# Stick-breaking attention: who carries the running product from one key chunk to the next

## The chip, the core and the metric

The kernel runs on one core of one Trainium2 chip. It is a single launch; the host only lays the arrays out. The metric is the device time of a run in microseconds (us). A profiled execution gives, beside its own time, the span from its first to its last instruction and a record of every instruction on the engines: TensorE (PE, with its weight loads PEld), VectorE (DVE), ScalarE (ACT), GpSimd (POOL) and the queue of SyncE (SP) that issues the DMAs.

## The reference, cut to what matters

One layer of a trunk: RMS norm with modulation, one wide input projection, a convolution branch, an attention branch, two gates, an output projection. Only the attention branch is touched. It is not a softmax: each query walks back over the earlier keys and leaves to each key a part of what is left.

```python
z = jnp.einsum("bqhd,bkhd->bhqk", qb, kb) * scale
mask = s_idx < t_idx
log_beta = jax.nn.log_sigmoid(z)
log_1m_beta = jnp.where(mask, log_beta - z, 0.0)
suffix = lax.cumsum(log_1m_beta, axis=3, reverse=True) - log_1m_beta
weights = jnp.where(mask, jnp.exp(log_beta + suffix), 0.0)
outs.append(jnp.einsum("bhqk,bkhd->bqhd", weights, vb))
```

Sequence 2048, 8 heads of 64, float32. The weight of a key is sigmoid(z) times the product of sigmoid(-z) over all keys between it and the query.

## The kernel before, in words

The sequence is laid out backwards, so that the product over the keys between becomes a running product from left to right. Heads are taken one after the other; in a head the queries come in 4 chunks `rc` of 512, and for each the key chunks `g` from `rc` to 3. So a head has ten **units** (rc, g): four on the diagonal (g = rc) and six off it, 80 in all. A unit has four query blocks `qb` of 128 rows.

`z_stage` (L783) does one query block of one unit: two matmuls give z in PSUM (L802, L803; the pool has two such buffers); ScalarE makes w = sigmoid(z) in SBUF (L805) and overwrites z by sigmoid(-z) in PSUM (L806); a scan on VectorE (L811, or L815 on the diagonal) writes the running product into columns 1 to 512 of `sc[qb]`, a tile of 513 columns of which there is one for each query block; GpSimd multiplies w by columns 0 to 511 of it (L818), and on the diagonal masks a 128x128 corner (L820). Column 0 holds what the chunk before has left. Off the diagonal a copy of one column on VectorE, L810, brings column 512 to column 0 before the scan. Its target is read by the product of the chunk before, so it cannot run until that product is done.

`av_stage` (L825) works on the unit before: TensorE transposes w into PSUM (L834, through the helper at L127), ScalarE casts it to `thi` (L842), VectorE makes the rest `tlo` (L843), and `av_mm` (L847) multiplies both by v and adds into `av`.

Between these stand filler matmuls: the dense projections of the merge gates, in steps of three matmuls (L763, tile `pd`), handed out over the quarters of the units by the list `due` (L949 to L954), which gives lighter units a little more. Of the fillers there are 416 steps, 402 of them inside the 302 quarters before `LAST`; in the last 18 quarters the first chunk of the next stage stands in their place.

The loop at L963 writes the order: Z(0), fillers, the held-back av_mm, fillers, Z(1), T(3), fillers, T(2), fillers, Z(2), fillers, AV(3), T(1), AV(2), T(0), Z(3), fillers, AV(1). With `pin[0]` set (L559) TensorE's matmuls keep this order (helpers `mm` and `tr`, L121 to L129). The queues of VectorE, ScalarE and GpSimd are ordered by the framework's planner, by what it takes to be ready and then by the place in the program; an instruction can stand in a queue well ahead of its place in the program. Each engine works its own queue off in order.

Of the kernel before, what the change touches and what calls it, by code (L numbers as in the profile page):

```python
# [22 lines left out]
CH = 512  # L23
NCH = SEQ // CH
# [21 lines left out]
def f(ap):  # L46
    return ap.bitcast(F32)
# [3 lines left out]
def trunk_kernel(  # L51
# [20 lines left out]
    nc = tc.nc  # L72
# [48 lines left out]
    def mm(*a, **k):  # L121
        i = nc.tensor.matmul(*a, **k)  # L122
        if pin[0]:
            tc.keep_in_program_order(i)
# [57 lines left out]
    with ExitStack() as s1:  # L182
# [193 lines left out]
        with tc.tile_pool(name="hx", reuse_waits="tile", bufs=1) as hx:  # L376
# [9 lines left out]
            for o in range(0, D, CH):  # L386
                s = slice(o, o + CH)
# [349 lines left out]
    with ExitStack() as s2:  # L737
# [37 lines left out]
        def load_q(h, rc):  # L775
            q1 = at.tile([P, CH], F32R, tag="q1", name="q1", bufs=2)
            q2 = at.tile([P, CH], F32R, tag="q2", name="q2", bufs=2)
            nc.sync.dma_start(f(q1), qst_d[h][rc])
            nc.sync.dma_start(f(q2[0:HD]), qst_d[h][rc][HD:P])
            nc.sync.dma_start(f(q2[HD:P]), qst_d[h][rc][0:HD])  # L780
            st[h, rc] = {"q": (q1, q2), "w": {}}

        def z_stage(h, rc, g, qb):  # L783
            diag = g == rc
            if qb == 0:
                if rc == 0:
                    kt[g] = at.tile([P, CH], F32R, tag=f"kt{g}", name=f"kt{g}")
                    nc.sync.dma_start(f(kt[g]), kst_d[h][g])
                    vt[g] = at.tile([P, 4, P], F32R, tag=f"vt{g}", name=f"vt{g}")
                    nc.sync.dma_start(f(vt[g]), vst_d[h][g])  # L790
                if diag:
                    nxt = (h, rc + 1) if rc + 1 < NCH else (h + 1, 0)
                    for hr in ((h, rc), nxt) if n_ == 0 else (nxt,):
                        if hr[0] < NH:
                            load_q(*hr)
            s_ = st[h, rc]
            q1, q2 = s_["q"]
            lo = qb * P if diag else 0
            zlo = min(lo, 256)
            qs = slice(qb * P, (qb + 1) * P)  # L800
            z = pz.tile([P, CH], F32, tag="z", name="z")
            mm(z[:, zlo:], q1[:, qs], kt[g][:, zlo:], start=True, stop=False)  # L802
            mm(z[:, zlo:], q2[:, qs], kt[g][:, zlo:], start=False, stop=True)  # L803
            w = at.tile([P, CH], F32, tag="w", name="w", bufs=7)
            nc.scalar.activation(out=w[:, lo:], in_=z[:, lo:], func=AF.Sigmoid, scale=HD ** -0.5)  # L805
            nc.scalar.activation(out=z[:, lo:], in_=z[:, lo:], func=AF.Sigmoid,  # L806
                                 scale=-HD ** -0.5)
            s = sc[qb]
            if not diag:
                nc.vector.tensor_copy(s[:, 0:1], s[:, CH:CH + 1])  # L810
                nc.vector.tensor_tensor_scan(  # L811
                    out=s[:, 1:], data0=z, data1=w, initial=s[:, 0:1],
                    op0=ALU.mult, op1=ALU.bypass)
            else:
                nc.vector.tensor_tensor_scan(  # L815
                    out=s[:, lo + 1:], data0=z[:, lo:], data1=tri[:, :CH - lo], initial=1.0,
                    op0=ALU.mult, op1=ALU.max)
            nc.gpsimd.tensor_tensor(out=w[:, lo:], in0=w[:, lo:], in1=s[:, lo:CH], op=ALU.mult)  # L818
            if diag:
                nc.gpsimd.affine_select(  # L820
                    out=w[:, lo:lo + P], in_=w[:, lo:lo + P], pattern=[[1, P]],
                    compare_op=ALU.is_gt, fill=0.0, base=0, channel_multiplier=-1)
            s_["w"][g, qb] = w

        def av_stage(h, rc, g, kb, v_):  # L825
# [137 lines left out]
        for n_, u in enumerate(units + [None]):  # L963
# [11 lines left out]
            def Z(qb):  # L975
                if u is not None:
                    z_stage(*u, qb)
# [118 lines left out]
```

## Time and profile before

| | us |
|---|---|
| median of three runs | 1952.85 |
| the three runs | 1952.85, 1944.73, 1953.7 |
| the profiled execution, its own time | 1947.37 |
| its span | 1945.6 |
| attention stage, about | 810 to 1602 of the span |

In the rows below, a group has its line, engine, operation, tiles (out<-in) and shape, then its count, its busy time, the mean of one in ns, and the idle time of its engine just before it with what ended that idle time. A row of the waits says who waited for whom, then us in total, how many times and the longest. A row of the chain gives start, duration and what; the chain is followed back from the last instruction to whatever released each one. A row of the windows gives a stretch, its length, and for each engine busy us and the count of instructions. A busy TensorE is not one at its peak, since its matmuls overlap and their ends are modelled.

### The profile page before, as it was taken

Reading aid. Unit: us, or ns where it says so; the run is one execution under the profiler, and the core shown is the slowest. Engines: PE = TensorE matmul, PEld = TensorE weight load, DVE = VectorE, ACT = ScalarE, POOL = GpSimd, SP = SyncE. Lnnn points to the kernel's source line nnn. Section 1 sums busy time; section 2 is a strip of 40 time slices with the busy share of each in tenths; the row PEclk is TensorE's granted clock in tenths of the full one; section 3 lists DMA queues with packets and bytes.
Section 4 is the critical chain, followed back from the end, with each engine's and each line's share of the span. In section 5 each row is a group of like instructions: output and inputs, shape, how many; then the busy total and the mean of one; then the engine's idle time right before and its main releaser. Section 6 shows DMA issues by size and latency. Waiting matters only on the chain.

```text
span 1945.6 us, 27211 instructions
## 1 busy us (share of the span) xinstructions
PE 1823.4 (94%) x9612; PEld 1517.2 (78%) x9612; DVE 1248.5 (64%) x1947; ACT 809.5 (42%) x1988; POOL 667.6 (34%) x739
## 2 busy tenths in 40 slices
PE   5889999999999989999998999999989889999999
PEld 4777898998988977777776777676767667888887
DVE  6864678787787445267776767676777797333341
ACT  3761122231221122266666666666667664010100
POOL 6441111011011144356465656455655551010100
PEclk9999999999999999999999999999999999999999
DMA  7335114052142444423232323131313246453532
GB/s 246 135 107 176 43 28 136 17 167 78 45 140 71 152 146 156 145 90 88 62 89 63 92 66 91 57 95 58 103 55 101 69 152 205 138 153 101 162 97 77
DMA packets 115290, 206.88 MB, mean 106 GB/s; under 512 B 15185, under 2 KB 27473, under 8 KB 115154
## 3 DMA queue, kind: packets, MB, share of 16 engines
q1 hardware_dynamic: 115154, 205.14, 33.8%
q8 instruction: 76, 1.25, 0.3%
q14 instruction: 60, 0.49, 0.1%
HBM read 133.78 MB, written 71.30 MB: 105 GB/s over the span
## 4 chain that ended last, share of the span: by engine, by line
PE 59%; DVE 16%; POOL 11%; issue 6%; DMA 5%; ACT 3%; SPq 1%; DVEq 0%; POOLq 0%; ACTq 0%
PE pd L122 33%; PE po L122 9%; POOL w L818 7%; PE p L122 7%; DVE sc L811 6%; PE av L122 4%; PE pT L127 3%; PE z L122 3%; DVE tlo L843 2%; POOL wlo L110 1%; DVE sc L815 1%; DMA gt<-ga 1%; ACT z L806 1%; DVE hhi L366 1%; DMA wl<-in_w_out_dram 1%
## 5 line engine op out<-in xcount | busy, mean ns | idle before, releaser
L818 POOL TENSOR_TENSOR w<-w,sc 128x512 f32<-128x512 f32 (+1 forms) x320 | 361.5, 1131 | 328.6 <-DVE sc L811 243.3
L122 PE MATMUL pd<-hhi,whi 128*128 128x512 f32 x1024 | 411.9, 402 | 0.0
L122 PE MATMUL pd<-hhi,wlo 128*128 128x512 f32 x1024 | 402.3, 393 | 0.0
L122 PE MATMUL pd<-hlo,whi 128*128 128x512 f32 x1024 | 401.7, 392 | 0.0
L110 POOL TENSOR_TENSOR wlo<-wl,whi 128x512 fp32r<-128x512 f32 x92 | 135.6, 1484 | 462.4 <-ACT whi L109 462.1
L811 DVE TENSOR_TENSOR_SCAN sc<-z,sc,w 128x512 f32<-128x512 f32 x192 | 244.0, 1276 | 53.1 <-ACT z L806 52.5
L805 ACT ACTIVATE w<-z 128x512 f32<-128x512 f32 (+1 forms) x320 | 171.8, 537 | 142.9 <-PE z L122 117.9
L122 PEld LDWEIGHTS pd<-hhi,wlo 128*128 128x128 f32 x1024 | 193.0, 189 | 41.9
L122 PE MATMUL pd<-whi,hhi 128*128 128x256 f32 x736 | 214.9, 292 | 8.1 <-DVE qn L287 8.1
L122 PEld LDWEIGHTS pd<-hhi,whi 128*128 128x128 f32 x1024 | 195.2, 191 | 33.8
L122 PE MATMUL pd<-whi,hlo 128*128 128x256 f32 x736 | 213.0, 291 | 8.5 <-POOL hlo L367 8.3
L122 PEld LDWEIGHTS pd<-hlo,whi 128*128 128x128 f32 x1024 | 193.6, 189 | 34.3
L122 PE MATMUL pd<-wlo,hhi 128*128 128x256 f32 x736 | 212.6, 289 | 0.2 <-POOL wlo L110 0.2
L122 PE MATMUL z<-kt,q 128*128 128x512 f32 (+2 forms) x640 | 195.9, 387 | 12.3 <-DVE sc L811 10.1
L842 ACT CAST thi<-pT 128x512 fp32r<-128x512 f32 (+1 forms) x320 | 165.1, 526 | 92.1 <-PE pT L127 88.7
L843 DVE TENSOR_TENSOR tlo<-pT,thi 128x512 fp32r<-128x512 f32 (+1 forms) x320 | 184.5, 596 | 13.4 <-ACT thi L842 11.0
L127 PE MATMUL pT<-ident,w 128*128 128x128 f32 x1088 | 174.8, 275 | 12.3 <-POOL w L818 12.1
L127 PEld LDWEIGHTS pT<-ident,w 128*128 128x128 f32 x1088 | 137.1, 140 | 49.3 <-POOL w L818 19.6
L806 ACT ACTIVATE z<-z 128x512 f32<-128x512 f32 (+1 forms) x320 | 171.5, 536 | 0.0
L122 PE MATMUL av<-tlo,vt 128*128 128x512 f32 (+1 forms) x320 | 126.1, 394 | 34.3 <-DVE tlo L843 30.5
L122 PEld LDWEIGHTS pd<-whi,hlo 128*128 128x128 f32 x736 | 143.8, 196 | 11.8 <-POOL hlo L367 11.2
L122 PEld LDWEIGHTS pd<-whi,hhi 128*128 128x128 f32 x736 | 144.9, 197 | 9.2 <-DVE qn L287 8.5
(274 smaller groups left out, 2994.3 us busy)
## 6 DMA issues: line engine op xcount, KB each, us to landing
wl<-in_w_in_dram SPq DMA_DIRECT2D x64, 256.0 KB, 2.9
wa<-in_w_ada_dram SPq DMA_DIRECT2D x24, 512.0 KB, 5.6
xt<-in_x_n_dram SPq DMA_DIRECT2D x16, 512.0 KB, 5.9
vst<-st SPq DMA_DIRECT2D x64, 128.0 KB, 1.9
kt<-kst SPq DMA_DIRECT2D x32, 256.0 KB, 2.8
vt<-vst SPq DMA_DIRECT2D x32, 256.0 KB, 2.8
q<-qst SPq DMA_DIRECT2D x32, 256.0 KB, 2.9
q<-qst SPq DMA_DIRECT2D x64, 128.0 KB, 3.1
```

The costliest lines, as they stand in the source:

```text
L110: (lo_eng or nc.gpsimd).tensor_tensor(out=lo[:, s], in0=wl, in1=f(hi[:, s]), op=ALU.subtract)
L122: i = nc.tensor.matmul(*a, **k)
L127: i = nc.tensor.transpose(*a)
L366: nc.vector.tensor_copy(hi, hf)
L805: nc.scalar.activation(out=w[:, lo:], in_=z[:, lo:], func=AF.Sigmoid, scale=HD ** -0.5)
L806: nc.scalar.activation(out=z[:, lo:], in_=z[:, lo:], func=AF.Sigmoid, scale=-HD ** -0.5)
L811: nc.vector.tensor_tensor_scan(out=s[:, 1:], data0=z, data1=w, initial=s[:, 0:1], op0=ALU.mult, op1=ALU.bypass)
L815: nc.vector.tensor_tensor_scan(out=s[:, lo + 1:], data0=z[:, lo:], data1=tri[:, :CH - lo], initial=1.0, op0=ALU.mult, op1=ALU.max)
L818: nc.gpsimd.tensor_tensor(out=w[:, lo:], in0=w[:, lo:], in1=s[:, lo:CH], op=ALU.mult)
L842: nc.scalar.copy(out=thi[:, :n], in_=pT[:, :n])
L843: nc.vector.tensor_tensor(out=tlo[:, :n], in0=pT[:, :n], in1=f(thi[:, :n]), op=ALU.subtract)
```

## The change

The copy on VectorE ahead of the scan goes. In its place GpSimd copies the same column, behind its own product (and behind the mask on the diagonal), in the unit that made the column, where a further key chunk follows (g < 3). Both kernels have 192 such copies: six of a head's ten units have a successor, times four query blocks, times eight heads.

```diff
             s = sc[qb]
             if not diag:
-                nc.vector.tensor_copy(s[:, 0:1], s[:, CH:CH + 1])
                 nc.vector.tensor_tensor_scan(
                     out=s[:, 1:], data0=z, data1=w, initial=s[:, 0:1],
                     op0=ALU.mult, op1=ALU.bypass)
...
                     compare_op=ALU.is_gt, fill=0.0, base=0, channel_multiplier=-1)
+            if g < NCH - 1:
+                nc.gpsimd.tensor_copy(s[:, 0:1], s[:, CH:CH + 1])
             s_["w"][g, qb] = w
```

## The prediction

> **What bounds the kernel now.** I read first the page's busy times, then the stage in which the touched lines run.
>
> ```profile
> span 1945.6 us, 27211 instructions
> ...
> PE 1823.4 (94%) x9612; PEld 1517.2 (78%) x9612; DVE 1248.5 (64%) x1947; ACT 809.5 (42%) x1988; POOL 667.6 (34%) x739
> ```
> ```profile
> 810.00:1602.00 792.00, 731.97 (x3700) 575.41 (x3699) 567.55 (x889) 524.79 (x1088) 448.26 (x544) 1.00 0.28 86
> ```
>
> TensorE is busy 94% of the span and 732 of the attention stage's 792 us, so at first sight nothing on VectorE (568 us) or GpSimd (448 us) can be worth more than 60 us. But its busy time is modelled, so I measure its pace where the chain of waits runs through TensorE alone:
>
> ```profile
> 1244.72 0.44 PE pT L127 x4
> 1245.16 0.47 PE z L122 x2
> 1245.62 1.39 PE pd L122 x6
> 1247.02 0.45 PE av L122 x2
> ```
>
> At full pace a 512-column matmul costs 0.23 us and a transpose 0.11. With the counts in the code a unit has a floor. Off the diagonal behind another such unit: z 8 matmuls 1.9, transposes 16 x 0.11 = 1.8, av 8 matmuls 1.8, and of the 402 filler steps over 75 units some 5.2 a unit, 15.5 matmuls or 3.6: 9.0 us in all. Off the diagonal behind a diagonal unit, with 10 transposes and narrower av: 8.0. Diagonal behind off-diagonal, with narrower z: 8.6. Diagonal behind diagonal (a head's first): 7.5. Now the ten units of the fifth head, each from its first z matmul to that of the next, in the order (0,0) (0,1) (0,2) (0,3) (1,1) (1,2) (1,3) (2,2) (2,3) (3,3):
>
> ```profile
> 1206.20:1215.40 9.20, 8.40 (x45) 6.80 (x44) 6.55 (x15) 5.18 (x13) 6.40 (x13) 1.00 0.53 163
> 1215.40:1225.30 9.90, 8.60 (x43) 6.42 (x42) 6.14 (x11) 7.04 (x14) 3.76 (x7) 1.00 0.29 89
> 1225.30:1236.70 11.40, 10.55 (x51) 7.59 (x51) 7.35 (x12) 6.99 (x13) 5.83 (x5) 1.00 0.14 47
> 1236.70:1247.00 10.30, 9.88 (x48) 7.24 (x48) 8.17 (x12) 6.64 (x12) 5.49 (x5) 1.00 0.05 6
> 1247.00:1255.60 8.60, 8.60 (x49) 7.08 (x48) 7.05 (x12) 5.75 (x13) 5.14 (x7) 1.00 0.28 90
> 1255.60:1265.70 10.10, 9.09 (x44) 7.04 (x43) 6.39 (x13) 7.88 (x16) 5.06 (x8) 1.00 0.20 63
> 1265.70:1275.80 10.10, 9.13 (x49) 7.26 (x49) 7.53 (x11) 6.50 (x12) 7.38 (x6) 1.00 0.28 89
> 1275.80:1284.30 8.50, 8.50 (x48) 6.98 (x48) 6.93 (x12) 5.75 (x13) 5.15 (x7) 1.00 0.28 87
> 1284.30:1292.80 8.50, 8.21 (x42) 6.61 (x41) 6.12 (x10) 6.86 (x14) 4.27 (x7) 1.00 0.27 80
> 1292.80:1301.80 9.00, 9.00 (x52) 7.56 (x52) 6.93 (x9) 5.11 (x13) 5.80 (x8) 1.00 0.31 87
> ```
>
> Above their floors they stand by 1.7, 1.9, 2.4, 1.3, 0.0, 2.1, 1.1, -0.1, 0.5 and 0.4: 11.3 us a head, some 90 in the stage. Those that reach their floor within half a microsecond are (1,1) and the last three. What the others share is seen in the chain, here inside (0,2):
>
> ```profile
> 1226.37 0.15 DVE sc L810
> 1226.53 1.21 DVE sc L811
> 1227.73 0.07 issue
> 1227.80 1.29 POOL w L818
> 1229.09 0.02 issue
> 1229.11 0.15 DVE sc L810
> ```
>
> Copy, scan, product, copy: the two engines take turns. One turn is 1229.11 - 1226.37 = 2.74 us, four are 11.0, against a floor of 9.0. The copy is ready when its product is done, so the planner has put it there, four query blocks ahead of the scan that needs it, and every scan or `tlo` behind it in VectorE's queue waits for a product that it has nothing to do with. The timeline has the proof that the second scan was ready:
>
> ```profile
> 1226.73 0.59 ACT L806 ACTIVATE z<-z 128x512 f32<-128x512 f32 x1
> ```
>
> Its input was there at 1227.32 and the scan before it ended at 1227.73; it began after the copy of 1229.11, about 1.4 late. All of it by groups and waits of the stage:
>
> ```profile
> L810 DVE COPY sc<-sc 128x1 f32<-128x1 f32 x192 | 27.5, 150 | 99.6 <-POOL w L818 98.4
> ```
> ```profile
> DVE sc L811 <- ACT z L806: 52.5, 45, 2.8
> ```
> ```profile
> PE av L122 <- DVE tlo L843: 30.5, 52, 1.2
> PE pT L127 <- POOL w L818: 12.1, 31, 1.0
> PE z L122 <- DVE sc L811: 10.1, 18, 1.0
> ```
>
> VectorE stands still 98.4 us at the copies and works 27.5 at them; TensorE's largest waits are for the `tlo` and the scans in that queue, and for the products that follow late scans.
>
> **The change part by part.** *Removed from VectorE*: 192 copies of 0.15 us and 98 us of standing at them. It is not the bound, so this counts only through TensorE's waits. I cost it by units that lack the wait. (2,3) follows a diagonal unit as (0,1) and (1,2) do, and no copy follows its products; it is 0.5 above its floor, they are 1.9 and 2.1. Brought to 0.5 they give 1.4 + 1.6 = 3.0 us a head, like for like. (0,2), (0,3) and (1,3) have no such twin. The first holds most of the waiting:
>
> ```profile
> DVE sc L810 <- POOL w L818: 3.9, 4, 1.4
> ```
>
> Nothing in these three excludes that they keep what they lose, nor that they come down to 0.5 as well, which would be 1.9 + 0.8 + 0.6 = 3.3. Between the ends I take 2.0: (0,2) falls from 2.4 to 1.0, the other two to 0.9 and 1.0, the rest going to scans that are truly late for T(3), since behind Z(3) stand 0.6 + 0.6 of ScalarE, 1.28 of scan and 1.3 of product, and only some 4.2 us of other matmuls. (0,0) waits as well for its z (1.7 above the floor); I take 0.5 of it, bounds 0 and 1.0. Sum 5.5 us a head, times 8 = 44; bounds 24 and (3.0 + 3.3 + 1.0) x 8 = 58.
>
> *Added to GpSimd*: 192 copies of 128x1. The trace before has none on this engine; the nearest rows:
>
> ```profile
> L147 POOL MEMSET invc<- 128x1 f32 x1 | 0.1, 99 | 0.0
> L92 POOL TENSOR_SCALAR nxt<-nxt 128x2 f32<-128x2 f32 x3 | 0.6, 191 | 0.3
> L820 POOL TENSOR_SCALAR_AFFINE_SELECT w<-w 128x128 f32<-128x128 f32 x128 | 38.5, 301 | 8.9
> ```
> ```profile
> L818 POOL TENSOR_TENSOR w<-w,sc 128x512 f32<-128x512 f32 x224 | 290.7, 1299 | 290.3 <-DVE sc L811 243.3 <-DVE sc L815 44.8 <-PE pT L127 1.0
> ```
>
> From below 0.10 (it writes as little, but reads nothing), from above 0.30; I take 0.19, the one-input row nearest in shape, with 0.07 for the step from one instruction to the next (the issue piece in the chain): 0.26. In all 192 x 0.26 = 50 us on an engine that stood 290 us waiting for scans ahead of its full products; that waiting is the cover. It is gone where scans come back to back: product and copy take 1.55, a scan 1.2, so the product that T(3) needs may come 0.26 late. Queued behind the copy are the next product, the `wlo` splits and the two memsets ahead of `tlo`; for the product wait T(3) to T(0). Copies stand in 48 units; one late product in each is 12.5 us, none 0. I take half, 6.
>
> *Added wait*: the scan now waits for GpSimd's copy, made a whole unit (8.5 to 11.4 us) before, while the copy ends about 1.5 behind its scan. Nothing is late by it. A second semaphore before each scan can cost an instruction of its own:
>
> ```profile
> L811 DVEq EVENT_SEMAPHORE  x25: 21/21/485, 835.9 to 1587.1; - x25
> ```
>
> that is 192 x 21 ns = 4 us on VectorE at most, and the 27.5 of the copies cover it. If not covered it costs those 4. No DMA is moved; the planner may order VectorE's and GpSimd's queues anew, TensorE's order is pinned.
>
> *A rule that speaks against it*: products will now run beside scans more often. The row: on GpSimd a two-input operation of 512 columns was once much slower than the 1299 ns of this stage:
>
> ```profile
> L110 POOL TENSOR_TENSOR w1l<-wl,w1h 128x512 fp32r<-128x512 f32 x4 | 7.2, 1810 | 1.8 <-DMA wl<-in_w_qkv_dram 1.8
> ```
> ```profile
> 1233.13 2.45 DVE L811 TENSOR_TENSOR_SCAN sc<-z,sc,w 128x512 f32<-128x512 f32 x2
> ...
> 1234.48 2.55 POOL L818 TENSOR_TENSOR w<-w,sc 128x512 f32<-128x512 f32 x2 [2.65 <-DVE sc L811]
> ```
>
> The Trainium skill, GPSIMD Engine Reference, section Specifications, says that GpSimd shares its SBUF interfaces with VectorE and that a VectorE instruction with two SBUF inputs contends with it. By that rule a scan that reads w and the carried column from SBUF might slow the product beside it. Here two products beside scans took 2.55, or 1.28 each: no slowing. I go by this row, and keep the other as a rival.
>
> *Sum*: 1947.4 - 44 + 6 = 1909.4. With the bounds of both costs: 1947.4 - 58 = 1889 to 1947.4 - 24 + 12.5 + 4 = 1940. The profiled execution is 5.5 below the median of the three runs and 2.6 above the lowest, so I say 1910.
>
> **The rivals.**
>
> *A, everything comes back.* Scan, product, transposes and `tlo` now overlap so well that every unit stays near its floor. For it: four of ten units do. Against it: T(3) follows Z(3) by hardly more than the latency worked out above. 90 us less would be 1857; with half a microsecond left in the six others, 58 less, and with TensorE's further waits in the last head up to 75: 1872 to 1889.
>
> *B, the z comes late anyway.* VectorE leaves the copies and waits for ScalarE instead, as it already does for 52.5 us. Only the like-for-like 24 us come, and 12.5 go to late products: 1935. Against it: inside (0,2) z was 1.4 early.
>
> *C, no change.* The copy's wait is replaced by the same wait elsewhere: the planner, by its own costs, still puts scans and `tlo` in an order in which one waits for the other's product. 1947, within 10 us. Against it: no data ties a query block's scan to another's product.
>
> *D, slower: GpSimd sets the pace.* Place: GpSimd's queue between two products. Price: 0.26 a copy, up to 0.30 + 0.07 = 0.37 by the upper row; if all 192 lie ahead of a product that a transpose waits for, 50 to 71 us, against 44 recovered. It decides from 44 / 192 = 0.23 us of TensorE's time lost per copy. 1947.4 - 44 + 71 = 1974 at the worst, 1960 in the middle. For it: products are already 12.1 us on TensorE's waits. Against it: 290 us of GpSimd's waiting in front of products.
>
> *E, contention.* Products beside scans go from 1.28 to 1.81. In a unit only the last product, 0.53 late, reaches T(3): 48 x 0.53 = 25 us given back, 1909 + 25 = 1934. This is what the rule above would make of it. Against it: the 2.55 for two.
>
> **How the numbers follow.** The forecast (1889 to 1935) has 0.55, A 0.12, B 0.12, C 0.09, D 0.08, E 0.04. A measurement of this kernel tells about 0.5%, 10 us, from no change. Faster by more than that: 0.55 + 0.12 + 0.11 + 0.03 = 0.81, since B and E have an edge within 10 us; same 0.11; slower 0.08. The range takes A's near part and the edge of C: 1872 to 1943. It leaves out D, most of C and A's far end. The faster cases alone would be 1872 to 1935.
>
> **What would show it.** Right: no copy in VectorE's queue and its 98 us of standing gone; TensorE's wait for `tlo` down from 30.5 us to under 12; (0,1), (0,2) and (1,2) shorter by 1.4 each; diagonal units as before; copies on GpSimd between 0.10 and 0.30. The term for late products is right if TensorE's 12.1 us of waiting for products stay under 20. Wrong: scans that wait for ScalarE by some 100 us in place of 52.5 (B), scans that wait for GpSimd's copies (C), transposes that wait for products by 40 us and more (D), products over 1.5 us beside scans (E).

## The result

The change makes the kernel faster: 1900.28 us (median of four runs, 1899.59 to 1906.09) against 1952.48 (median of four, 1944.73 to 1953.7), a ratio of 0.9747 with a 95% interval of 0.9716 to 0.9779. The prediction was 1910. A second comparison on another occasion gave 1903.41 and 0.9741 (0.9723 to 0.9759).

The page of the kernel after, with the parts that answer to those shown of before. Line numbers past the removed copy are off by one: the scan is now L810, the product L817, the mask L819, the copy on GpSimd L823, `thi` L843, `tlo` L844. In the experiments they shift again by a line or two; there the names of the tiles tell which row is meant.

```profile
span 1898.2 us, 27437 instructions
...
PE 1805.2 (95%) x9612; PEld 1522.1 (80%) x9612; DVE 1230.8 (65%) x1755; ACT 807.6 (43%) x1988; POOL 693.8 (37%) x931
...
PE 69%; DVE 11%; POOL 6%; issue 6%; DMA 4%; ACT 3%; SPq 0%; DVEq 0%; ACTq 0%; POOLq 0%
```

TensorE has the same 9612 matmuls. VectorE has 192 instructions fewer, GpSimd 192 more. The chain that ended last runs through TensorE for 69% of the span; in the page of before it was 59%, with 16% on VectorE and 11% on GpSimd:

```profile
PE 59%; DVE 16%; POOL 11%; issue 6%; DMA 5%; ACT 3%; SPq 1%; DVEq 0%; POOLq 0%; ACTq 0%
```

Where the time came from is seen in the windows: first the attention stage after, then what follows it, then what followed it before.

```profile
810.00:1553.00 743.00, 711.24 (x3700) 577.43 (x3699) 552.00 (x698) 521.55 (x1088) 474.45 (x735) 1.00 0.30 91
```
```profile
1553.00:1898.00 345.00, 339.29 (x1481) 276.32 (x1479) 135.15 (x200) 47.27 (x79) 17.70 (x16) 1.00 0.44 133
```
```profile
1602.00:1945.00 343.00, 338.57 (x1478) 275.79 (x1476) 135.44 (x199) 46.62 (x78) 17.04 (x15) 1.00 0.44 134
```

The same 3700 matmuls take 743 us in place of 792. The span is 47.4 us shorter: 49 come from this stage, and what follows it is 2 us longer than it was. The ten units of the fifth head, cut in the same way as before:

```profile
1182.30:1190.70 8.40, 8.37 (x45) 6.79 (x44) 6.10 (x11) 5.18 (x13) 6.66 (x15) 1.00 0.60 177
1190.70:1199.50 8.80, 8.05 (x43) 6.46 (x42) 6.01 (x8) 6.98 (x14) 4.88 (x10) 1.00 0.38 102
1199.50:1208.90 9.40, 9.40 (x52) 7.91 (x51) 7.66 (x9) 6.79 (x13) 6.23 (x9) 1.00 0.18 58
1208.90:1217.90 9.00, 9.00 (x48) 7.37 (x47) 7.33 (x9) 6.43 (x12) 5.62 (x7) 1.00 0.06 12
1217.90:1226.50 8.60, 8.60 (x49) 7.06 (x48) 6.86 (x9) 5.74 (x13) 5.42 (x10) 1.00 0.26 86
1226.50:1235.70 9.20, 8.84 (x44) 7.12 (x43) 6.56 (x10) 7.76 (x16) 5.61 (x11) 1.00 0.22 67
1235.70:1245.60 9.90, 8.84 (x49) 7.25 (x48) 6.93 (x9) 6.48 (x12) 7.51 (x8) 1.00 0.29 92
1245.60:1254.20 8.60, 8.60 (x49) 7.08 (x48) 6.82 (x9) 5.75 (x13) 5.41 (x10) 1.00 0.27 83
1254.20:1262.70 8.50, 8.14 (x41) 6.52 (x41) 5.94 (x9) 6.83 (x14) 4.38 (x8) 1.00 0.27 83
1262.70:1271.70 9.00, 9.00 (x53) 7.57 (x52) 6.88 (x9) 5.15 (x13) 5.78 (x8) 1.00 0.33 85
```

The head takes 89.4 us in place of 95.6, and the first seven heads, measured in the same way, each shrink by 5.3 to 7.1 us. (1,1), (2,2), (2,3) and (3,3), which stood near their floors, are within 0.1 of what they were; the six others shrink by 0.8, 1.1, 2.0, 1.3, 0.9 and 0.2. Inside (0,2), where two engines took turns, the timelines of VectorE and GpSimd now read:

```profile
1199.59 1.28 DVE L810 TENSOR_TENSOR_SCAN sc<-z,sc,w 128x512 f32<-128x512 f32 x1 [0.65 <-ACT z L806]
1201.61 1.28 DVE L810 TENSOR_TENSOR_SCAN sc<-z,sc,w 128x512 f32<-128x512 f32 x1 [0.74 <-ACT z L806]
```
```profile
1200.95 1.30 POOL L817 TENSOR_TENSOR w<-w,sc 128x512 f32<-128x512 f32 x1 [0.78 <-DVE sc L810]
1202.31 0.18 POOL L823 COPY sc<-sc 128x1 f32<-128x1 f32 x1
```

The second scan begins at 1201.61, while the product of the first (1200.95 to 1202.25) still runs; what it waited for is its own z.

### The profile page after: what moved, and what is told of

Same layout as the page of the kernel before. It is cut to its first block, busy times and chain, and to the rows that moved or that the text cites. A ratio compares the mean times of both kernels' runs of the same rounds, so it can differ in the third digit from the quotient of the medians.

```text
span 1898.2 us, 27437 instructions
## 1 busy us (share of the span) xinstructions
PE 1805.2 (95%) x9612; PEld 1522.1 (80%) x9612; DVE 1230.8 (65%) x1755; ACT 807.6 (43%) x1988; POOL 693.8 (37%) x931
## 4 chain that ended last, share of the span: by engine, by line
PE 69%; DVE 11%; POOL 6%; issue 6%; DMA 4%; ACT 3%; SPq 0%; DVEq 0%; ACTq 0%; POOLq 0%
PE pd L122 38%; PE po L122 9%; PE p L122 7%; PE av L122 5%; PE pT L127 5%; PE z L122 4%; POOL w L817 3%; DVE sc L810 2%; POOL wlo L110 1%; DVE hhi L366 1%; DMA gt<-ga 1%; DMA wl<-in_w_out_dram 1%; ACT z L806 1%; DVE tlo L844 1%; PE pt L127 1%
## 5 line engine op out<-in xcount | busy, mean ns | idle before, releaser
L817 POOL TENSOR_TENSOR w<-w,sc 128x512 f32<-128x512 f32 (+1 forms) x320 | 361.8, 1131 | 251.7 <-DVE sc L810 178.8
L810 DVE TENSOR_TENSOR_SCAN sc<-z,sc,w 128x512 f32<-128x512 f32 x192 | 244.8, 1279 | 91.9 <-ACT z L806 84.5
L844 DVE TENSOR_TENSOR tlo<-pT,thi 128x512 fp32r<-128x512 f32 (+1 forms) x320 | 183.9, 597 | 34.7 <-ACT thi L843 32.3
L843 ACT CAST thi<-pT 128x512 fp32r<-128x512 f32 (+1 forms) x320 | 165.3, 527 | 61.0 <-PE pT L127 57.5
L127 PE MATMUL pT<-ident,w 128*128 128x128 f32 x1088 | 172.2, 273 | 10.5 <-POOL w L817 10.2
L122 PEld LDWEIGHTS pd<-wlo,hhi 128*128 128x128 f32 x736 | 145.9, 198 | 0.7 <-POOL wlo L110 0.4
```

Source lines behind the costliest of these rows:

```text
L127: i = nc.tensor.transpose(*a)
L810: nc.vector.tensor_tensor_scan(out=s[:, 1:], data0=z, data1=w, initial=s[:, 0:1], op0=ALU.mult, op1=ALU.bypass)
L843: nc.scalar.copy(out=thi[:, :n], in_=pT[:, :n])
L844: nc.vector.tensor_tensor(out=tlo[:, :n], in0=pT[:, :n], in1=f(thi[:, :n]), op=ALU.subtract)
```

## The experiments

Two theories were held against each other. **Standing**: the copy on VectorE cost what it did because it stood in VectorE's queue, far ahead of its scan, until GpSimd's product was done. **Busy**: VectorE gained by being rid of 192 instructions of work, and anything that relieves it would do the same. Each experiment's edit is against the kernel named; all ratios are to the kernel before.

**The changed kernel again**, as the yardstick of the next three.

> The changed kernel itself, as the yardstick for the three variants beside it. Both theories: 1895 to 1907 us, VectorE standing less than 5 us at anything that belongs to the carried column.

Measured 1903.41 us, ratio 0.9741 (0.9723 to 0.9759). The scans wait 2.1 us in all for the copies on GpSimd.

**Pinned on VectorE.** The kernel before, with one call around the copy that keeps it from being queued ahead of the VectorE instruction before it in the program:

```diff
-                nc.vector.tensor_copy(s[:, 0:1], s[:, CH:CH + 1])
+                tc.keep_in_program_order(
+                    nc.vector.tensor_copy(s[:, 0:1], s[:, CH:CH + 1]))
```

> The copy stays on VectorE, in its old place in the program, but is pinned behind the VectorE instruction ahead of it there, so that it cannot stand four query blocks early. Theory 'standing' (the loss came from where the copy stood in the queue, not from which engine makes it): VectorE still works 27.5 us at 192 copies, stands under 15 us at them, and the time is 1898 to 1912. Rival 'busy' (VectorE's own 27.5 us and the relief of that engine made the gain): 1940 to 1955, as before.

Measured 1905.47 us, 0.976 (0.9733 to 0.9787). Its group, and a wait of TensorE:

```profile
L811 DVE COPY sc<-sc 128x1 f32<-128x1 f32 x192 | 26.2, 137 | 0.3
```
```profile
PE pT L127 <- POOL w L819: 9.5, 22, 1.3
```

VectorE still makes all 192 copies, 26.2 us of work, and stands 0.3 us at them where it stood 99.6. In the trace a copy now stands one to four instructions ahead of its scan in VectorE's queue; in the kernel before it was five to fourteen, and the copy began 8 us ahead of the scan in the mean. The gain is there, and its interval overlaps that of the changed kernel. So the gain needs no copy on GpSimd.

**Behind the product, on VectorE.** The changed kernel with the copy back on VectorE in the new place of the program:

```diff
             if g < NCH - 1:
-                nc.gpsimd.tensor_copy(s[:, 0:1], s[:, CH:CH + 1])
+                nc.vector.tensor_copy(s[:, 0:1], s[:, CH:CH + 1])
```

> The copy is on VectorE, but in the new place in the program, right behind the product. Theory 'standing': the planner puts it where it put the old one, VectorE stands 80 to 130 us at it, and the time is 1942 to 1962. Rival 'place' (the new place in the program made the gain, whatever the engine): 1895 to 1910.

Measured 1956.21 us, 1.0023 (1.001 to 1.0035).

```profile
L823 DVE COPY sc<-sc 128x1 f32<-128x1 f32 x192 | 28.2, 151 | 104.1 <-POOL w L817 102.6
```

The standing is back, with the copies six or more instructions ahead of their scans again, and the whole gain is gone: the place in the program is not what counts.

**The work back, without the standing.** The changed kernel, with a copy of the same column on VectorE into a tile that nobody reads, ahead of GpSimd's:

```diff
+        junk = at.tile([P, 1], F32, name="junk")
...
             if g < NCH - 1:
+                nc.vector.tensor_copy(junk, s[:, CH:CH + 1])
                 nc.gpsimd.tensor_copy(s[:, 0:1], s[:, CH:CH + 1])
```

> The changed kernel, with 192 further copies of the same column on VectorE into a tile that nobody reads; each needs only the scan ahead of it on VectorE, so it is work of 0.15 us without standing. Theory 'standing': 0 to 8 us over the changed kernel, 1897 to 1910. Rival 'busy': at least half of the gain goes back, 1922 or more.

Measured 1905.22 us, 0.9757 (0.9742 to 0.9772).

```profile
L824 DVE COPY junk<-sc 128x1 f32<-128x1 f32 x192 | 28.5, 148 | 3.6
```

28.5 us of work on VectorE cost 1.8 us by the medians, and the intervals overlap. With the pinned copy this settles it between the two theories: work of this size on VectorE is nearly free here, standing is not.

**On ScalarE.** The changed kernel with `nc.scalar.copy(out=s[:, 0:1], in_=s[:, CH:CH + 1])` in place of GpSimd's copy.

> The copy goes to ScalarE, in the new place behind the product. Theory 'standing': any other engine than the product's own has to stand for the product in its queue; ScalarE stands 60 to 130 us at the copies, its w, z and thi come later, and the time is 1925 to 1965. Rival 'relief' (what counts is that VectorE has no copy): 1897 to 1912.

Measured 1974.18 us, 1.0122 (1.0101 to 1.0143): slower than before, and over the upper end that was expected.

```profile
L823 ACT COPY sc<-sc 128x1 f32<-128x1 f32 x192 | 35.7, 191 | 152.3 <-POOL w L817 127.4 <-DVE sc L814 23.9
L810 DVE TENSOR_TENSOR_SCAN sc<-z,sc,w 128x512 f32<-128x512 f32 x192 | 244.9, 1280 | 145.9 <-ACT z L806 142.6 <-POOL w L819 1.7 <-POOL w L817 0.7
```

(The two rows are from different engines' groups.) VectorE is relieved just as much as in the changed kernel, and yet the time is lost: ScalarE now stands 152.3 us, and the scans wait 142.6 for the z that it makes. Part of the standing is for diagonal scans: in query blocks 1 to 3 of a diagonal unit the product starts at a later column and does not read column 0, so that there, in every one of these kernels, the copy has only the scan to wait for; elsewhere it is held by the product. The expectation had the mechanism and was low on the size. ScalarE's instructions lie ahead of the scan and, with `thi`, ahead of `tlo`. TensorE's waits show both:

```profile
PE z L122 <- DVE sc L810: 28.1, 37, 1.3
PE av L122 <- DVE tlo L844: 23.4, 41, 1.0
```

In the changed kernel these two are 4.0 and 10.1 (shown further down). The matmuls of z wait for a buffer that a late scan still holds, 24 us more, and av waits for `tlo` 13 us more. That is 37 of the 71 us lost against the changed kernel; the rest was not taken apart.

**Half and half.** Query blocks 0 and 1 keep the copy on VectorE, 2 and 3 have it on GpSimd:

```diff
             if not diag:
+                if qb < 2:
+                    nc.vector.tensor_copy(s[:, 0:1], s[:, CH:CH + 1])
...
-            if g < NCH - 1:
+            if g < NCH - 1 and qb >= 2:
                 nc.gpsimd.tensor_copy(s[:, 0:1], s[:, CH:CH + 1])
```

> Query blocks 0 and 1 keep the copy on VectorE, 2 and 3 have it on GpSimd. Theory 'standing': VectorE stands 35 to 65 us at the 96 copies left and the time lies between the two kernels, 1915 to 1935. If one standing copy a unit is enough to set the two engines to taking turns: 1940 or more.

Measured 1929.41 us, 0.9885 (0.9864 to 0.9907), and the kernel before beside it 1951.86.

```profile
L811 DVE COPY sc<-sc 128x1 f32<-128x1 f32 x96 | 13.1, 147 | 48.6 <-POOL w L819 48.6
```

Half of the standing (48.6 us of 98.4), and 22 us of some 50 gained: in these three points the loss goes with the standing, about half a microsecond of time for one of standing. That is a sum, and not so in each unit. In the mean over the heads (0,1) and (1,2) are as long as in the kernel before (9.4 and 9.6 us), so the two copies left cost them all that four did, while (0,2) falls from 11.6 to 10.2 and (0,3) from 10.1 to 9.4.

**Four copies on GpSimd.** The changed kernel with `for _ in range(4):` ahead of GpSimd's copy, so that 576 more are made.

> The changed kernel with each of GpSimd's copies made four times, 576 more of 185 ns. The step of the prediction that late products cost half of 48 x 0.26 us: three more copies cost three times as much and more, 18 to 40 us over the changed kernel, and TensorE's wait for products goes from 10 to over 25 us. If GpSimd's waiting for scans covers copies altogether: under 6 us over the changed kernel.

Measured 1918.26 us, 0.9828 (0.981 to 0.9847).

```profile
PE pT L127 <- POOL w L817: 20.0, 24, 2.2
```
```profile
DVE sc L810 <- POOL sc L824: 17.9, 12, 2.5
```

The ratio is 0.0087 above the changed kernel's 0.9741, some 17 us by the ratios for three more copies each: just under the 18 that a price in proportion had as its lower end, and well over the 6 of full cover. TensorE's wait for products goes from 10.2 to 20.0, under the 25 that were expected, and in 12 places a scan has to wait for a carried column. The price is not spread over the units: in the mean over the heads (0,2) goes from 9.5 to 10.6 us and (1,3) from 9.8 to 10.7, and no other unit moves by more than 0.2. So in those two GpSimd's slack ends somewhere between one copy and four, and in the others it covers four copies, or nearly so.

## Why the prediction was right, point by point

The time came out 10 us under 1910, inside the range and inside the likeliest case's own bounds (1889 to 1935).

*The bound, and where the loss lay.* Right. The units that stood at their floor did not move, the others went towards it. The floors themselves were rough: each was taken with 15.5 filler matmuls, but the timeline has 18 in (0,0), (0,2), (1,2) and (3,3) of the fifth head and 15 in the rest. Two small sums are off as well, and move nothing: the falls named for (0,2), (0,3) and (1,3) add to 1.9 and not 2.0, and rival A's half microsecond left in six units is 60 us less rather than 58.

*The removed standing.* Right in mechanism, shown by the pinned copy, by the copy back on VectorE and by the halves. The term was 44 us (5.5 a head); the stage gave 49 and the fifth head 6.2. That the total came so near is in part luck, since its parts were mis-sized in both directions. The like-for-like units, (0,1) and (1,2), were to give 3.0 a head and gave 1.1 + 0.9 = 2.0. For (1,2) the fault is in the floor: it has 18 filler matmuls where (2,3) has 15. With their own counts and the same 0.23 and 0.11 us, (1,2) came from 1.6 above its floor to 0.6, which is where (2,3) stands (0.6 before, 0.7 after); (0,1) came from 2.2 to 1.1 and stopped short of it. (0,2), (0,3) and (1,3) were taken at 2.0 between 0 and 3.3, and gave 2.0 + 1.3 + 0.2 = 3.5, over the upper bound, since the first two ended at 9.4 and 9.0, within 0.2 of floors by their own counts (9.4 and 8.9) and not half a microsecond above, which I had put as the best. (0,0) gave 0.8 for 0.5. Of the unit signs, 1.4 each for (0,1), (0,2) and (1,2), the direction came, and the sizes were 1.1, 2.0 and 0.9. The groups of the stage after:

```profile
L810 DVE TENSOR_TENSOR_SCAN sc<-z,sc,w 128x512 f32<-128x512 f32 x192 | 244.8, 1279 | 91.9 <-ACT z L806 84.5 <-POOL w L819 2.0 <-POOL w L817 1.9
```
```profile
L823 POOL COPY sc<-sc 128x1 f32<-128x1 f32 x192 | 37.5, 195 | 5.6
L817 POOL TENSOR_TENSOR w<-w,sc 128x512 f32<-128x512 f32 x224 | 290.7, 1298 | 223.8 <-DVE sc L810 178.8 <-DVE sc L814 44.5
```
```profile
PE pT L127 <- POOL w L817: 10.2, 21, 1.4
PE av L122 <- DVE tlo L844: 10.1, 21, 0.7
PE z L122 <- DVE sc L810: 4.0, 5, 1.2
```

Scans wait for z for 84.5 us in place of 52.5, so rival B's mechanism was there, short of the 100 named as its sign; it did not reach TensorE, whose own wait for scans fell from 10.1 to 4.0. TensorE's wait for `tlo` fell from 30.5 to 10.1, under the 12 that were named as the sign.

*The copy on GpSimd.* 195 ns in the mean where I took 190, from the one-input row nearest in shape. Product and copy were to take 1.55 us; where the next product follows at once, inside (0,2), it begins 1.50 behind the one before:

```profile
1206.18 1.30 POOL L817 TENSOR_TENSOR w<-w,sc 128x512 f32<-128x512 f32 x1 [1.66 <-DVE sc L810]
1207.54 0.18 POOL L823 COPY sc<-sc 128x1 f32<-128x1 f32 x1
1207.68 1.29 POOL L817 TENSOR_TENSOR w<-w,sc 128x512 f32<-128x512 f32 x1
```

*The late product.* This is the term that failed: 6 us (half of 48 x 0.26), and hardly anything is to be found of it. TensorE waits 10.2 us for products, less than the 12.1 of before, and the pinned kernel, with no copy on GpSimd at all, still has 9.5. The sign for this term, a wait under 20, came, but it would have come with no price at all too. The step assumed that scans come back to back ahead of T(3) in half the units. In the stage after, GpSimd still stands 223.8 us waiting for scans ahead of its full products, which leaves room for one copy; with four a price is seen, and in two of a head's ten units alone. That makes the 10 us: some 5 from the units and 6 from this term, less the 2 by which what follows the stage became longer.

*The added wait.* The second semaphore did come:

```profile
L810 DVEq EVENT_SEMAPHORE  x178: 21/21/21, 835.0 to 1538.9; - x178
```

178 of them in place of 25, 21 ns each, 3.7 us. That nothing would be late by the added wait was nearly so: the scans stood 1.9 and 2.0 us for GpSimd's products and a mask, as in their group's row above, and once, for 1.9 us, for the carried column itself:

```profile
DVE sc L810 <- POOL sc L823: 1.9, 1, 1.9
```

*The rule on shared SBUF interfaces.* The Trainium skill, GPSIMD Engine Reference, section Specifications, says that GpSimd contends with a VectorE instruction that has two SBUF inputs. Beside these scans, whose z lies in PSUM, no slowing is seen. Added up from the timelines, full products overlap off-diagonal scans for 78 us where it was 53, and their mean is 1298 ns where it was 1299; the 60 that run at least 0.6 us beside such a scan take 1.29 us each in the mean. Rival E is out. Whether the carried column counts as an input in that rule, no run here shows. The row that I went by showed less than I took from it: its two scans end at 1235.58 and its products run from 1234.48 to 1237.03, so only the first of them ran beside a scan.

*Rivals C and D*: the scans' waits for GpSimd are the few microseconds above, so the copy's wait did not come back elsewhere; GpSimd as the pace is seen only with more than one copy, in two units. *Rival A* would have needed 1872 to 1889; the fifth head keeps 5 us above its floors.

## What to carry to other kernels

Look in an in-order queue for an instruction that is small and early: its own work (150 ns) is not the price, but everything behind it while it stands. Either give it to the engine whose result it waits for, where it has nothing to wait for, or pin it behind the work that can go first; here both gave the same 2.5%. To see what removal is worth, give the stage's units their floors at full matmul pace rather than reading the bound engine's busy share. The 732 busy us of 792 left room for 60, the floors for 90, and 49 came, which both allow; but the busy time itself fell to 711 with the same matmuls, so part of the loss had been hidden in it, and only the floors told in which units the loss lay. Count each unit's own matmuls for this.

## What was not expected

The same copy behind the same product had no cost that could be seen on GpSimd, and on ScalarE the kernel took 22 us more than before (1974.18 against 1951.86), though ScalarE was less busy in the stage than VectorE (525 us against 568 of 792). So the load of an engine did not decide. What stands behind the copy in the queue fits better, on ScalarE both the z of the scans and the `thi` ahead of `tlo`; of the 71 us lost against the changed kernel, TensorE's two waits explain 37, and the rest stays open.
